# Order by hand held to the end of the second projection; copies of the last norm factors' rows and banks of the output product moved

## The chip, the cores and the metric

The kernel runs on one core of one Trainium2 chip. The metric is the device time of one execution in microseconds (us), the median of three runs. The engines in the profile: PE is TensorE (matmuls), PEld its weight loads, DVE is VectorE, ACT is ScalarE, POOL is GpSimd, SP is SyncE, which here issues DMAs.

## The reference

One layer that joins a gMLP mixer and a Mamba-2 mixer, in float32, with D = S = 1024 and one sequence. Its end, which the change touches, is:

```python
y_b = rms_norm(yz, ssm_norm_w.reshape(SSM_GROUPS, -1)).reshape(b, s, SSM_D_INNER)   # 2048 wide, 8 groups
merged = jax.nn.sigmoid(g_a) * (y_a @ w_proj_a) + jax.nn.sigmoid(g_b) * (y_b @ w_proj_b)
x = x + gate[:, None, :] * (merged @ w_out)
return rms_norm(x, final_norm_w)
```

## The kernel before

All of the product `y_b @ w_proj_b` is called the second projection here. It is done by seven products of half size (Strassen in Winograd's form) in the order p1, p2, p5, p3, p6, p7, p4. Each product runs over k = 0 to 7, and one pair (product, k) is a unit; `units` numbers them u = 0 to 55. A unit (`multiply`) is 12 matmuls of 128x128 by 128x512: four banks of PSUM, and on each bank the three parts of a product in split precision, where every operand is a high part (`bh`, a cast) and a low part (`bl`, what the cast left). p1, p6, p7 and p4 gather on the banks `x`, p2, p5 and p3 on the banks `y`; p3 goes on from p5's sums, and p6, p7 and p4 from what is in `x`.

After each unit `ahead(u)` issues the loads of unit u + 6 (on SP) and the operands of unit u + 4. `operands` makes the norm of a row block of y_b (`y_norm`, for p1, p2, p5 and p3), the differences that Winograd's form needs (`yn`), the cast to the high part on ScalarE and the low part on VectorE. `bh` and `bl` are rings of four, so the cast of unit u + 4 writes where unit u is read. When a product is done, its banks are copied or added to a sum (`c11`, `c`, p5's and p3's copies, and `p` in the trace for the sums that p6 and p7 are added to): p1's and p2's by `emptied_banks`, ahead of `ahead(u)`; the others at the loop's end, with high priority. From p3 on, every second unit has a `merged`: one piece of the merged rows from such a sum and two pieces loaded by `gate_load` (`tg`, `ma`), which ends as a high and a low part (`mh`, `ml`), operands of the output product. p4's banks are read by `merged` directly. During p7 and p4 pieces of w_out are loaded and split (`wo_load`, `wo_parts`).

VectorE, ScalarE and GpSimd run their instructions in the order in which the program has them after scheduling. While `hand[0]` is true, the wrapper class `Engine` pins each instruction to program order; when it is false, the scheduler orders by its own estimates. It is set true at the last pair of the input products and, before, false at u = 23, the end of p5. TensorE's matmuls of this projection are pinned in any case.

`post3` makes the norm factors' rows of one group pair: a transpose on TensorE into a bank of p2's set (`rows_bank`), a copy on VectorE (`cwt`, `tri`), and a store to `rs_d`, from which `y_load` reads rows (`rb`) for `y_norm`. In p1 it is called for groups 6 and 7.

`places_of` gives the banks of each set by `free`, the list of the banks in the order in which the work before gives them up; here it is [1, 7, 2, 3, 0, 4, 5, 6]. The pool `ps4` behind the loop has two tags: `pj` (two tiles of two banks, the output product's) and `one` (four tiles of one bank, its last row block). The output product starts with k = 4 to 7 and 0 to 3 (`KO`) on row blocks 4 and 5, whose operands are `merged`'s pieces (b, 1). `room` is the list of tags that `slot_tile` takes from the front.

Of the kernel before, what the change touches and what calls it, by code (L numbers as in the profile page):

```python
# [8 lines left out]
F32 = mybir.dt.float32  # L9
# [7 lines left out]
P = 128  # L17
D = 1024
S = 1024
KT = D // P  # L20
NCH = S // P
NG = 8
# [13 lines left out]
def hybrid_kernel(  # L36
# [7 lines left out]
    hand = [False]  # L44
# [13 lines left out]
    V, A, G, PE = Engine(nc.vector), Engine(nc.scalar), Engine(nc.gpsimd), nc.tensor  # L58
    ctx.enter_context(nc.allow_non_contiguous_dma(reason="small parameter vectors"))

    x, out = x[0], out[0]
# [33 lines left out]
    def f32(t):  # L95
        return t.bitcast(F32)
# [80 lines left out]
    with tc.tile_pool(name="p0", bufs=1, reuse_waits="tile") as p0:  # L177
# [257 lines left out]
        sums = {(6, 8): [(last_sums, 0)], (7, 2): [(last_sums, 1)], (7, 5): [(last_sums, 2)]}  # L435
# [47 lines left out]
    free, at_bank = [], {}  # L483
# [12 lines left out]
    def numbered(pool, c):  # L496
        for b in range(8):
            pool.tile([P, 512], F32, name=f"{c}{b}_0", tag=f"{c}{b}")
# [676 lines left out]
    groups = [Group(g) for g in range(NG)]  # L1175
# [36 lines left out]
    def ring(n):  # L1212

        return [room.pop(0) for _ in range(n)], [0]
# [20 lines left out]
    war_r, wah_r, wal_r = [], [], []  # L1235
# [144 lines left out]
    tha_r, ea_r, y1_r, ym_r = (ring(c) for c in (4, 3, 2, 2))  # L1380
# [59 lines left out]
    def banks(name, c):  # L1440
        return [psb.tile([P, 512], F32, name=f"{name}{j}", tag=f"q{places_of[c][j]}") for j in range(4)]
# [12 lines left out]
    def slot_tile(name, dt=F32):  # L1454
        tag = room.pop(0)
        t = hp.tile([P, 512], dt, name=name, tag=tag)
        tags_of[name] = tag
        return t

    def give(name):  # L1460
        room.append(tags_of.pop(name))
# [79 lines left out]
    def multiply(u, ps):  # L1541
        nm, k = units[u]
        first = nm in ("p1", "p2", "p5")
        a, (bh, bl) = aops.pop(u), bops.pop(u)
        for j in range(4):
            js = slice(j * P, (j + 1) * P)
            for n, (v, r) in enumerate(((0, bh), (0, bl), (1, bh))):
                pin(PE.matmul(ps[j], a[:, v, js], r, start=first and n + k == 0, stop=n == 2 and k == KT - 1,  # L1548
                              skip_group_check=not first))
# [3 lines left out]
    def gate_load(b, h):  # L1553
        hs = slice(h * 512, (h + 1) * 512)
        th, ma = gate_slot(f"tg{b}_{h}"), gate_slot(f"ma{b}_{h}")
        load(th, th_d[(KT + b) * P : (KT + b + 1) * P, hs])
        load(ma, mt_d[b][:, hs])
        gates[b, h] = th, ma
# [4 lines left out]
    def m_slot(name):  # L1563
        if m_sl:
            if not places:
                pool, b = m_sl.pop(0)
                t = pool.tile([P, 3, 512], F32R, name=f"m{name}", tag="sl", bufs=b)
                places.extend(t[:, i] for i in range(3))
            return places.pop(0)
        return places.pop(0) if places else slot_tile(name, F32R)  # L1570
# [6 lines left out]
    def merged(b, h, c, name):  # L1577

        th, ma = gates.pop((b, h))
        V.scalar_tensor_tensor(th, th, 1.0, c, op0=ALU.add, op1=ALU.mult)  # L1580
        V.tensor_add(th, th, ma)
        hi, lo = m_slot(f"mh{b}_{h}"), m_slot(f"ml{b}_{h}")
        if name:
            give(name)
        A.copy(hi, th)
        V.tensor_sub(lo, th, f32(hi))
        mhl[b, h] = hi, lo
# [3 lines left out]
    def ahead(u):  # L1591
        if u + LOAD < len(units):
            loads(u + LOAD)
        if u + LEAD < len(units):
            operands(u + LEAD)
# [3 lines left out]
    def ya_free():  # L1599

        while emptied[0] < KT and left[0] <= 3 * (KT - 1 - emptied[0]):
            room.extend(ya_tags[emptied[0]])
            emptied[0] += 1
# [3 lines left out]
    n = 0  # L1607
# [8 lines left out]
            loads(n - 1)  # L1616
    draw(left[0] + 1)
    ya_free()
    for tags in (war_r[0][0][:2], wah_r[0][0][2:], wal_r[0][0][2:], tha_r[0], y1_r[0], ym_r[0]):
        room.extend(tags)  # L1620
    ps2.__exit__(None, None, None)
    ps3 = tc.tile_pool(name="ps3", bufs=1, space=PSUM, reuse_waits="tile")
    psb = ps3.__enter__()
    numbered(psb, "q")
    places_of = {"x": free[:4], "y": free[4:]}
    wo, wor = {}, {}
    KO = (4, 5, 6, 7, 0, 1, 2, 3)

    def wo_load(k):
        wor[k] = [[slot_tile(f"wo{v}{k}_{c}", F32R) for v in "hl"] for c in range(2)]  # L1630
        for c in range(2):
            load(f32(wor[k][c][1]), wo_d[k][:, c * 512 : (c + 1) * 512])

    def wo_parts(k):
        for hi, lo in wor[k]:
            A.copy(hi, f32(lo))
            V.tensor_sub(lo, f32(lo), f32(hi))
        wo[k] = wor.pop(k)

    psx = psy = None  # L1640
    sums, more = [], []

    def emptied_banks(nm):
        for j in range(4):
            if nm == "p1":
                t = slot_tile(f"c11_{j}")
                A.copy(t, psx[j])
                more.append((j, 0, t, f"c11_{j}"))
            else:
                V.tensor_add(more[j][2], more[j][2], psy[j])  # L1650

    for u, (nm, k) in enumerate(units):
        if k == 0:
            if nm == "p1":
                psy = banks("yp2", "y")
                psx = banks("x", "x")
                rows_bank[0] = lambda name: psy[int(name[2:]) - 6]
            elif nm == "p5":
                psy = banks(f"y{nm}", "y")
            elif nm == "p6":  # L1660
                room.extend(rb_r[0])
            ps = psy if nm in ("p2", "p5", "p3") else psx
        multiply(u, ps)
        if u < 16 and k == KT - 1:
            emptied_banks(nm)
        ahead(u)
        if nm == "p1" and k in (4, 5):
            groups[NG - 6 + k].post3(True)
        if k % 2 and nm in GATES:
            gate_load(GATES[nm][0] + k // 2, GATES[nm][1])  # L1670
        if nm in ("p7", "p4") and k % 2 == 0:
            n = k // 2 + (4 if nm == "p4" else 0)
            kept = 2 * (16 - len(mhl)) - len(places) - 3 * len(m_sl)
            if len(room) >= 4 + kept and len(wor) + len(wo) < KT:
                wo_load(KO[len(wor) + len(wo)])
        if nm == "p4" and k % 2 and wor:
            wo_parts(next(iter(wor)))
        if k % 2 and more and u > 23:
            merged(*more.pop(0))
        if u == 23:  # L1680
            hand[0] = False
        if u > 15 and k == KT - 1:
            for j in range(4):
                with tc.high_priority():
                    if nm in ("p5", "p3"):
                        t = slot_tile(f"{nm}_{j}")
                        A.copy(t, psy[j])
                        sums.append(t)
                    elif nm == "p6":
                        V.tensor_add(sums[4 + j], sums[4 + j], psx[j])  # L1690
                        more.append((j, 1, sums[4 + j], f"p3_{j}"))
                    elif nm == "p7":
                        V.tensor_add(sums[j], sums[j], psx[j])
                        more.append((4 + j, 1, sums[j], f"p5_{j}"))
                    elif nm == "p4":
                        merged(4 + j, 0, psx[j], None)
    room.extend(bh_r[0] + bl_r[0])
    for n in KO:
        if n not in wo:
# [4 lines left out]


    ps4 = ctx.enter_context(tc.tile_pool(name="ps4", bufs=1, space=PSUM, reuse_waits="tile"))

    def pj_tile(name):
        return ps4.tile([P, 1024], F32, name=name, tag="pj", bufs=2)
# [4 lines left out]
    def inv_root(sq):  # L1714

        y, t, v = sq[:, 2:3], sq[:, 3:4], sq[:, 1:2]
        V.tensor_scalar(t, sq[:, 0:1], 1.0 / D, EPS, op0=ALU.mult, op1=ALU.add)
        V.tensor_scalar(y.bitcast(I32), t.bitcast(I32), -0.5, float(0x5F3759DF), op0=ALU.mult, op1=ALU.add)
        V.tensor_scalar_mul(v, t, -0.5)
        for _ in range(3):  # L1720
            V.scalar_tensor_tensor(t, y, y, v, op0=ALU.mult, op1=ALU.mult)
            V.scalar_tensor_tensor(y, t, 1.5, y, op0=ALU.add, op1=ALU.mult)
        return y
# [24 lines left out]
    for n, t in enumerate(tiles):  # L1748
# [22 lines left out]
        if last:  # L1771
            V.scalar_tensor_tensor(sq[:, 0:1], part[:, 0:1], part[:, 1:2], part[:, 2:3], op0=ALU.add, op1=ALU.add)
            y = inv_root(sq)
# [4 lines left out]
        else:  # L1778
            V.tensor_add(r, pw, xr)  # L1779
            A.activation(xr, r, AF.Square, accum_out=sq[:, 0:1])  # L1780
            y = inv_root(sq)
# [35 lines left out]
```

## Time and profile before

| | |
|---|---|
| time, median of 3 runs | 1432.4 us (1431.67 to 1433.11) |
| profiled execution | 1435.1 us |
| its span, first to last instruction | 1433.4 us |
| granted TensorE clock, mean | 0.995 |
| busy: PE, DVE, ACT, POOL | 97%, 72%, 54%, 14% |

The profiled execution has its own time, 2.7 us over the median; the rows of the profile belong to it. The second projection stands from about 1161 us to 1335 us of the span, the output product behind it. A matmul's row in the timeline gives start, length and in brackets the idle time before it with what ended that; a window's PEclk is the granted clock in that stretch, 1.00 for full speed.

### The profile page before, as it was taken

The numbers are of one execution on the slowest core, as the hardware profiler recorded it, in microseconds if no ns is written. First come the engines' busy times: TensorE is split into PE (matmuls) and PEld (weight loads), VectorE is DVE, ScalarE is ACT, GpSimd is POOL, SyncE is SP. The second block draws the span as 40 slices with busy tenths as digits, with TensorE's granted clock in tenths as the row PEclk, the third lists the DMA queues.
The fourth block names the chain that finished last, engine by engine and source line by source line (L and its number), as shares of the span: only waits on it lengthen the run. The fifth ranks groups of instructions, "written<-read, shape, count | busy, mean of one in ns | idle before, by whom it ended". The sixth has DMA issues, their size and how long they took to land.

```text
span 1433.4 us, 20485 instructions
## 1 busy us (share of the span) xinstructions
PE 1394.2 (97%) x7087; PEld 1152.3 (80%) x7087; DVE 1030.4 (72%) x1827; ACT 781.1 (54%) x1438; POOL 205.7 (14%) x190
## 2 busy tenths in 40 slices
PE   8999999999999999999999999999999998899997
PEld 6688888888888888888887888878888886687786
DVE  4686677777667888788877884768777757938443
ACT  6664576566656665555665555667767533325211
POOL 0000000000000000000010100048878820000000
PEclk9999999999999999999999999999999999999999
DMA  8552333333332677586676764789689488877331
GB/s 267 157 164 89 118 118 102 104 104 109 111 110 89 206 224 225 180 263 200 194 239 200 221 189 147 248 306 323 254 293 318 147 272 311 291 244 281 121 118 74
DMA packets 260524, 277.08 MB, mean 193 GB/s; under 512 B 13596, under 2 KB 210628, under 8 KB 260420
## 3 DMA queue, kind: packets, MB, share of 16 engines
q1 hardware_dynamic: 179396, 195.37, 43.3%
q10 hardware_dynamic: 81024, 80.40, 16.1%
q8 instruction: 56, 0.92, 0.2%
q14 instruction: 48, 0.39, 0.1%
HBM read 191.40 MB, written 84.31 MB: 192 GB/s over the span
## 4 chain that ended last, share of the span: by engine, by line
PE 77%; DMA 7%; DVE 7%; ACT 3%; issue 2%; POOL 2%; SPq 1%; ACTq 0%; POOLq 0%; DVEq 0%
PE xuz L585 6%; PE xcb L585 6%; PE po L90 6%; PE xx L585 6%; PE xz L585 5%; PE xg L585 5%; PE pma L90 3%; PE yuz L585 3%; PE xv L585 3%; PE ycb L585 3%; PE yx L585 3%; PE yp L1548 3%; PE yz L585 3%; PE yg L585 2%; PE yi L90 2%
## 5 line engine op out<-in xcount | busy, mean ns | idle before, releaser
L796 POOL TENSOR_TENSOR wog<-wog,gb 128x1024 f32<-128x1024 f32 x8 | 22.5, 2809 | 727.3 <-DMA wbr<-in_w_proj_b_dram 615.5
L56 ACT ACTIVATE dcy<-dcy,nacs 128x128 f32<-128x128 f32 x256 | 78.4, 389 | 34.4 <-POOL dcy L56 16.2
L56 POOL TENSOR_SCALAR_AFFINE_SELECT dcy<-dcy 128x1024 f32<-128x1024 f32 x32 | 37.4, 1169 | 106.0 <-ACT ea L56 105.9
L908 ACT ACTIVATE ac<-ac 128x1024 f32<-128x1024 f32 x32 | 34.0, 1062 | 20.2 <-DVE ac L906 20.1
L1780 ACT ACTIVATE xr<-r 128x1024 f32<-128x1024 f32 x7 | 7.4, 1061 | 66.8 <-issue 39.0
L90 PE MATMUL pma<-yh,wah 128*128 128x512 f32 x128 | 43.2, 419 | 0.1
L90 PE MATMUL pma<-yh,wal 128*128 128x512 f32 x128 | 42.8, 415 | 0.0
L56 DVE TENSOR_TENSOR ym<-yn,ea 128x512 f32<-128x512 f32 (+1 forms) x32 | 19.9, 623 | 30.2 <-PE yn L90 30.0
L56 POOL TENSOR_TENSOR yz<-y,sl 128x512 f32<-128x512 f32 x32 | 41.2, 1287 | 0.6
L56 ACT ACTIVATE ea<-dcy 64x512 f32<-64x512 f32 x64 | 40.2, 629 | 1.8 <-DMA dcy<-acs_d 1.3
L56 DVE TENSOR_TENSOR dcy<-dcy,pc 128x1024 f32<-128x1024 f32 x32 | 39.0, 1219 | 2.6 <-PE pc L93 1.4
L90 PE MATMUL pma<-yl,wah 128*128 128x512 f32 x128 | 40.0, 393 | 0.0
L1770 POOL TENSOR_TENSOR r<-r,fnw 128x256 f32<-128x256 f32 (+1 forms) x3 | 2.8, 917 | 254.2 <-ACT xr L1769 254.2
L56 POOL TENSOR_TENSOR y<-y,ym 128x512 f32<-128x512 f32 (+1 forms) x32 | 36.7, 1146 | 12.7 <-DVE ym L56 12.6
L906 DVE SCALAR_TENSOR_TENSOR ac<-c2x,cwt,ac 128x1023 f32<-128x1023 f32 (+2 forms) x24 | 31.8, 1325 | 9.0 <-ACT ac L904 7.1
L1779 DVE TENSOR_TENSOR r<-po,xr 128x1024 f32<-128x1024 f32 x7 | 8.6, 1225 | 41.2 <-PE po L90 41.1
L90 PE MATMUL yi<-dcy,xd 128*64 128x128 f32 x512 | 35.0, 279 | 0.9 <-DVE xe L56 0.6
L906 DVE SCALAR_TENSOR_TENSOR ac<-c2cb,cwt,ac 128x1023 f32<-128x1023 f32 (+2 forms) x24 | 30.6, 1275 | 7.1 <-ACT ac L904 7.0
L90 PE MATMUL sp<-xe,bn 128*128 128x256 f32 x112 | 32.7, 409 | 0.0
L90 PEld LDWEIGHTS yi<-dcy,xd 128*64 128x64 f32 x512 | 27.3, 136 | 5.3 <-issue 2.9
L906 DVE SCALAR_TENSOR_TENSOR ac<-c1cb,cwt,ac 128x1023 f32<-128x1023 f32 (+2 forms) x24 | 30.6, 1276 | 0.7 <-ACT ac L904 0.7
L906 DVE SCALAR_TENSOR_TENSOR ac<-c1x,cwt,ac 128x1023 f32<-128x1023 f32 (+2 forms) x24 | 30.6, 1277 | 0.0
(2847 smaller groups left out, 4400.2 us busy)
## 6 DMA issues: line engine op xcount, KB each, us to landing
sl<-s_d SPq DMA_DIRECT2D x32, 768.0 KB
s_d<-ac ACTq DMA_DIRECT2D x32, 512.0 KB
dcy<-acs_d SPq DMA_DIRECT2D x32, 512.0 KB
aw<-in_ada_w_dram SPq DMA_DIRECT2D x16, 512.0 KB
wbr<-in_w_proj_b_dram SPq DMA_DIRECT2D x64, 128.0 KB
wb_d<-wbb ACTq DMA_DIRECT2D x32, 256.0 KB
wb_d<-wbc ACTq DMA_DIRECT2D x32, 256.0 KB
yb_d<-yz ACTq DMA_DIRECT2D x32, 256.0 KB
```

The source lines that it names most:

```text
L56: return lambda *a, **k: tc.keep_in_program_order(f(*a, **k))
L90: pin(PE.matmul(acc, l, r, start=first, stop=last))
L585: pin(PE.matmul(ps, lw[:, k * P : (k + 1) * P], r[k], start=first and n + k == 0, stop=n == 2 and k == 3, skip_group_check=not first))
L796: G.tensor_mul(w, w, gb)
L906: V.scalar_tensor_tensor(ac[:, s:], cc[:, : S - s], conv_wt[:, 3 - s, i : i + 1], ac[:, s:], op0=ALU.mult, op1=ALU.add)
L908: A.activation(ac, ac, AF.Silu)
L1548: pin(PE.matmul(ps[j], a[:, v, js], r, start=first and n + k == 0, stop=n == 2 and k == KT - 1, skip_group_check=not first))
L1770: G.tensor_mul(r[:, cs], r[:, cs], fnw[:, cs])
L1779: V.tensor_add(r, pw, xr)
L1780: A.activation(xr, r, AF.Square, accum_out=sq[:, 0:1])
```

## The change

`hand[0]` stays true to the end of p4. All emptying of banks is now in `emptied_banks`, without high priority and ahead of `ahead(u)` for every product but p4, whose banks are emptied after the loop. `merged` is taken from the list ahead of the emptying and issued at the end of the unit. `post3` is called after p1's units k = 2 and 3, ahead of `ahead`. The banks are fixed: x is (1, 2, 3, 0) and y is 4 to 7. In `ps4` four tiles of the tag `one` are asked for first, which puts `pj` on banks 4 to 7. One group of tags goes to the end of `room`.

```diff
-    for tags in (war_r[0][0][:2], wah_r[0][0][2:], wal_r[0][0][2:], tha_r[0], y1_r[0], ym_r[0]):
+    for tags in (war_r[0][0][:2], wah_r[0][0][2:], wal_r[0][0][2:], y1_r[0], ym_r[0], tha_r[0]):
...
-    places_of = {"x": free[:4], "y": free[4:]}
+    places_of = {"x": (1, 2, 3, 0), "y": range(4, 8)}
...
             else:
-                V.tensor_add(more[j][2], more[j][2], psy[j])
+                merged(4 + j, 0, psx[j], None)
...
         multiply(u, ps)
-        if u < 16 and k == KT - 1:
+        if nm == "p1" and k in (2, 3):
+            groups[NG - 4 + k].post3(True)
+        due = more.pop(0) if k % 2 and more and u > 23 else None
+        if k == KT - 1 and nm != "p4":
             emptied_banks(nm)
         ahead(u)
-        if nm == "p1" and k in (4, 5):
-            groups[NG - 6 + k].post3(True)
...
-        if k % 2 and more and u > 23:
-            merged(*more.pop(0))
-        if u == 23:
-            hand[0] = False
-        if u > 15 and k == KT - 1:
-            for j in range(4):
-                with tc.high_priority():
...
+        if due:
+            merged(*due)
+    emptied_banks("p4")
+    hand[0] = False
...
+    for n in range(4):
+        ps4.tile([P, 512], F32, name=f"one{n}_0", tag="one", bufs=4)
```

The branches of the removed block for p5, p3, p6 and p7 stand unchanged in `emptied_banks`, together with p2's.

On VectorE around the operands of p3's k = 2 and 3 (`p3bl_12000` is the low part of k = 2; `yn` rows are norms and differences, those of line 1520, 1534 and 1523 belong to p6 and p7), before:

```order
L1580 SCALAR_TENSOR_TENSOR tg_0_12024<-tg_0_12024,c_3_11620 128x512
L1534 TENSOR_TENSOR yn_0_11508<-yn_0_11508,yn_1_11721 128x512
L1523 TENSOR_TENSOR yn_0_11249<-yn_1_11721,yn_0_11249 128x512
L1520 TENSOR_TENSOR yn_1_11818<-yn_1_12015,yn_1_11818 128x512
L1487 SCALAR_TENSOR_TENSOR yn_1_12050<-yn_1_12050,par_140,rb_1_12048 128x512
L1520 TENSOR_TENSOR yn_1_11746<-yn_1_11946,yn_1_11746 128x512
L1534 TENSOR_TENSOR yn_0_11590<-yn_0_11590,yn_1_11792 128x512
L1523 TENSOR_TENSOR yn_0_11327<-yn_1_11792,yn_0_11327 128x512
L56 TENSOR_TENSOR p3bl_12000<-yn_1_11946,p3bh_11999 128x512
```

And after, at the same place:

```order
L56 TENSOR_TENSOR p3bl_11973<-yn_1_11918,p3bh_11972 128x512
L56 SCALAR_TENSOR_TENSOR yn_1_11946<-yn_1_11946,par_140,rb_1_11944 128x512
L56 TENSOR_TENSOR p3bl_12000<-yn_1_11946,p3bh_11999 128x512
L56 SCALAR_TENSOR_TENSOR yn_1_11967<-yn_1_11967,par_140,rb_1_11944 128x512
L56 TENSOR_TENSOR p3bl_12029<-yn_1_11967,p3bh_12028 128x512
```

Before, differences of p6 and p7 and a step of `merged` stand between the norm and the low part of a p3 unit; after, norm and low part stand side by side, and the others come later.

On VectorE at the end of p6 (`p` with `x` are the adds that empty p6's banks, `p7bl` the low parts of p7's operands, the first three for k = 0 to 2), before:

```order
L1527 TENSOR_TENSOR p7bl_12329<-yn_0_11244,p7bh_12328 128x512
L1527 TENSOR_TENSOR p7bl_12348<-yn_0_11249,p7bh_12347 128x512
L1690 TENSOR_TENSOR p_0_12217<-p_0_12217,x_11416 128x512
L1527 TENSOR_TENSOR p7bl_12371<-yn_0_11256,p7bh_12370 128x512
L1690 TENSOR_TENSOR p_1_12219<-p_1_12219,x_11417 128x512
```

And after:

```order
L56 TENSOR_TENSOR yn_0_11672<-yn_0_11672,yn_1_11868 128x512
L56 TENSOR_TENSOR yn_0_11244<-yn_1_11698,yn_0_11244 128x512
L56 TENSOR_TENSOR p7bl_12329<-yn_0_11244,p7bh_12328 128x512
L56 TENSOR_TENSOR yn_0_11249<-yn_1_11721,yn_0_11249 128x512
L56 TENSOR_TENSOR p7bl_12348<-yn_0_11249,p7bh_12347 128x512
L56 TENSOR_TENSOR yn_0_11256<-yn_1_11746,yn_0_11256 128x512
L56 TENSOR_TENSOR p7bl_12371<-yn_0_11256,p7bh_12370 128x512
L56 TENSOR_TENSOR p_0_12204<-p_0_12204,x_11416 128x512
L56 TENSOR_TENSOR p_1_12206<-p_1_12206,x_11417 128x512
L56 TENSOR_TENSOR p_2_12208<-p_2_12208,x_11418 128x512
L56 TENSOR_TENSOR p_3_12210<-p_3_12210,x_11419 128x512
```

The differences that p7 needs stand now right ahead of its low parts, six instructions of p7's k = 0 to 2 are ahead of the first add, and the four adds stand together.

On VectorE in p1, the difference of the two orders where the rows of groups 6 and 7 are copied (`cwt`, `tri`):

```order
+L56 COPY cwt<-yp_11412 8x128
 L56 SCALAR_TENSOR_TENSOR yn_0_11434<-yn_0_11434,par_140,rb_0_11432 128x512
-L56 TENSOR_TENSOR p1bl_11491<-yn_0_11434,p1bh_11490 128x512
+L56 TENSOR_TENSOR p1bl_11494<-yn_0_11434,p1bh_11493 128x512
 L56 TENSOR_TENSOR p1a_11436<-p1r_11437,p1a_11436 128x512
+L56 COPY tri<-yp_11413 8x128
 L56 SCALAR_TENSOR_TENSOR yn_0_11458<-yn_0_11458,par_140,rb_0_11432 128x512
```

The two copies stand now ahead of the operands of p1's k = 6 and 7; before, they stood behind those of p2's k = 0 and 1.

More of the change, by code (lines that the diff above doesn't have):

```diff
@@ L1624, in hybrid_kernel @@
     numbered(psb, "q")
-    places_of = {"x": free[:4], "y": free[4:]}
+    places_of = {"x": (1, 2, 3, 0), "y": range(4, 8)}
+    assert all(b > 3 for b in free[6:])
     wo, wor = {}, {}
@@ L1648, in emptied_banks @@
                 more.append((j, 0, t, f"c11_{j}"))
+            elif nm == "p2":
+                V.tensor_add(more[j][2], more[j][2], psy[j])
+            elif nm in ("p5", "p3"):
+                t = slot_tile(f"{nm}_{j}")
+                A.copy(t, psy[j])
+                sums.append(t)
+            elif nm == "p6":
+                V.tensor_add(sums[4 + j], sums[4 + j], psx[j])
+                more.append((j, 1, sums[4 + j], f"p3_{j}"))
+            elif nm == "p7":
+                V.tensor_add(sums[j], sums[j], psx[j])
+                more.append((4 + j, 1, sums[j], f"p5_{j}"))
             else:
-                V.tensor_add(more[j][2], more[j][2], psy[j])
+                merged(4 + j, 0, psx[j], None)
     for u, (nm, k) in enumerate(units):
@@ L1677, in hybrid_kernel @@
             wo_parts(next(iter(wor)))
-        if k % 2 and more and u > 23:
-            merged(*more.pop(0))
-        if u == 23:
-            hand[0] = False
-        if u > 15 and k == KT - 1:
-            for j in range(4):
-                with tc.high_priority():
[L1685 to L1696, printed above, removed]
+        if due:
+            merged(*due)
+    emptied_banks("p4")
+    hand[0] = False
     room.extend(bh_r[0] + bl_r[0])
```

## The prediction

> **What bounds the kernel now.** I read first the head of the page, then the waits of TensorE in the last third of the span, then TensorE's timeline at each of these waits, and last VectorE's timeline just before them.
>
> ```profile
> span 1433.4 us, 20485 instructions
> PE 1394.2 (97%) x7087; PEld 1152.3 (80%) x7087; DVE 1030.4 (72%) x1827; ACT 781.1 (54%) x1438; POOL 205.7 (14%) x190
> ```
>
> TensorE is busy for 97% of the span: it sets the time, and what can be won is its idle time and the stretches at half clock. The waits of TensorE from 1100 us on (total, times, longest):
>
> ```profile
> PE yp L1548 <- DVE p3bl L56: 6.7, 3, 4.3
> PE yp L1548 <- issue: 4.4, 1, 4.4
> PE po L90 <- DVE tg L1580: 2.2, 1, 2.2
> PE yp L1548 <- DVE tri L56: 1.9, 1, 1.9
> PE x L1548 <- DVE p L1690: 0.6, 2, 0.4
> ```
>
> They sum to 15.8 us, nearly all of them VectorE's doing. TensorE's timeline has them at these places (start, duration, engine, line, operation; in brackets the idle time before it):
>
> ```profile
> 1161.63 0.39 PE L1548 MATMUL x<-p1bh,p1a 128*128 128x512 f32 x1
> 1163.44 0.61 PE L1548 MATMUL x<-p1bh,p1a 128*128 128x512 f32 x2
> 1166.16 0.61 PE L1548 MATMUL x<-p1bh,p1a 128*128 128x512 f32 x2
> 1186.61 0.50 PE L1548 MATMUL yp<-p2bh,p2a 128*128 128x512 f32 x1 [1.88 <-DVE tri L56]
> 1212.37 0.76 PE L1548 MATMUL yp<-p5bh,p5a 128*128 128x512 f32 x1 [4.37 <-issue]
> 1246.35 0.80 PE L1548 MATMUL yp<-p3bl,p3a 128*128 128x512 f32 x1 [4.33 <-DVE p3bl L56]
> 1253.10 0.79 PE L1548 MATMUL yp<-p3bl,p3a 128*128 128x512 f32 x1 [2.17 <-DVE p3bl L56]
> 1268.20 0.39 PE L1548 MATMUL x<-p6bh,p6a 128*128 128x512 f32 x1
> 1289.96 0.39 PE L1548 MATMUL x<-p7bh,p7a 128*128 128x512 f32 x1
> 1312.93 0.39 PE L1548 MATMUL x<-p4bh,p4a 128*128 128x512 f32 x1
> 1335.28 0.39 PE L90 MATMUL po<-woh,mh 128*128 128x512 f32 x1
> 1339.00 0.50 PE L90 MATMUL po<-woh,mh 128*128 128x512 f32 x1 [2.20 <-DVE tg L1580]
> ```
>
> From 1163.44 to 1166.16 run 12 matmuls, one unit: 2.72 us, and a product of eight units 21.76 us undisturbed. p6 shows just that (1268.20 to 1289.96). p7 takes 22.97 and p4 22.35. The windows behind three of the gaps, and behind the one of 1.88 (length; busy time and count of PE, PEld, DVE, ACT, POOL; granted clock; DMA share; GB/s):
>
> ```profile
> 1212.20:1215.60 3.40, 3.23 (x8) 2.58 (x9) 3.22 (x6) 0.04 (x1) 0.00 (x0) 0.50 1.03 410
> 1246.30:1249.70 3.40, 3.35 (x8) 2.67 (x9) 3.40 (x6) 1.22 (x2) 0.00 (x0) 0.50 0.01 4
> 1253.10:1256.50 3.40, 3.40 (x8) 2.72 (x9) 3.40 (x6) 0.00 (x0) 0.00 (x0) 0.50 0.10 42
> 1184.80:1188.20 3.40, 1.59 (x7) 1.33 (x8) 2.36 (x5) 1.63 (x4) 0.00 (x0) 1.00 0.47 144
> ```
>
> So a long gap costs itself and 1.7 us more, half of 3.4 us at half clock; the gap of 1.88 us drew no such stretch, that of 2.17 us did.
>
> **The prices on VectorE.**
>
> ```profile
> 1165.74 0.15 DVE L56 TENSOR_SCALAR ssq<-pq 128x4 f32<-128x4 f32 x1
> 1186.28 0.27 DVE L56 COPY tri<-yp 8x128 f32<-8x128 f32 x1
> 1208.75 0.75 DVE L56 SCALAR_TENSOR_TENSOR yn<-yn,par,rb 128x512 f32<-128x512 f32 x1
> 1209.53 0.69 DVE L56 TENSOR_TENSOR yn<-yn,yn 128x512 f32<-128x512 f32 x1
> 1210.98 0.69 DVE L56 TENSOR_TENSOR p5bl<-yn,p5bh 128x512 fp32r<-128x512 f32 x1 [0.76 <-ACT p5bh L56]
> 1211.59 2.48 DVE L56 TENSOR_TENSOR c<-c,yp 128x512 f32<-128x512 f32 x4
> 1213.98 0.75 DVE L56 SCALAR_TENSOR_TENSOR yn<-yn,par,rb 128x512 f32<-128x512 f32 x1
> 1243.81 0.68 DVE L1520 TENSOR_TENSOR yn<-yn,yn 128x512 f32<-128x512 f32 x1
> 1244.41 0.69 DVE L1534 TENSOR_TENSOR yn<-yn,yn 128x512 f32<-128x512 f32 x1
> 1245.61 0.69 DVE L56 TENSOR_TENSOR p3bl<-yn,p3bh 128x512 fp32r<-128x512 f32 x1
> ```
>
> From start to start: a p5 unit (norm, difference, wait for ScalarE's cast, low part) 2.84 us (1208.75 to 1211.59); a p3 unit without one step of 0.78 then 2.06; the four adds that empty a set of banks 2.39 (1211.59 to 1213.98), the first after some 0.7; one more plain difference 0.60 (1243.81 to 1244.41). A p6 unit (difference, cast, low part, difference) is 2.66 and a p7 unit 2.06, a p4 unit (the low part alone) 0.6. A `merged` (two steps, cast, low part) has a p5 unit's shape: 2.84. These are estimates from the rows above.
>
> **The change part by part.** The rows of groups 6 and 7 move from p1's k = 4, 5 to k = 2, 3, two units sooner and ahead of the operands of p1's k 6 and 7 instead of behind those of p2's k 0 and 1. The copy of `tri` at 1186.28, for which p2 finds one of its banks still unread, then comes about 5 us sooner, and the wait of 1.88 us goes. In its place p1's fourth bank is now bank 0, last read by VectorE at 1165.74 to 1165.89, while p1 comes to it 9 matmuls, 2.04 us, after its start at 1161.63: a new wait of some 2.2 us (1165.9 less 1163.67). Neither counts: p5 starts when VectorE's adds at 1211.59 have emptied the first bank, and these stand behind the operands of p5's k 0 to 2 as before; p2's end, 4.37 us ahead, has room for either. Were that cover gone, 0.3 us would be the net. Worth 0, and the 4.37 us gap with its half clock stays. The stores of these rows go out sooner too, and SP, which now stands 7.9 us for one of them ahead of the row loads, stands shorter; TensorE waits for none of those loads, so this is worth 0 as well.
>
> ```profile
> SPq L99 <- DMA rs_d<-cwt: 7.9, 1, 7.9
> 1298.97 6.92 DMA p4a<-wb_d
> SPq L99 <- DVE tg L1581: 12.9, 2, 8.8
> ```
>
> The copies that empty p5's banks, on ScalarE, also lose their priority and stand behind the casts of p3's k 0 to 2. The last of these waits for p5's k 6 to end, 2.72 us before the copies can begin, so ScalarE is free by then; 0, at most the 0.6 of one cast.
>
> p3 is the gain. Its low parts now wait behind p6's and p7's differences, the rows before 1245.61; in the new order each p3 unit has its norm and its low part side by side. The cast of unit u + 4 waits for TensorE's end of unit u (a ring of four), so VectorE is done some 1.5 us after that, about 6 us ahead of need. p3 shrinks from 32.5 us (1235.7 to 1268.20, the start being p5's 1212.37 + 1.7 + 21.76) to 21.8: −10.7 us. It starts p6 at about 1257.6.
>
> VectorE is then late. p3's k 1 ends at 1212.37 + 1.7 + 10 × 2.72 = 1241.3, so k 5's operands end at 1242.8. What stands behind them in order: merged to 1245.6, p3's k 6 and 7 to 1249.8, merged to 1252.6, p6's k 0 and 1 to 1257.9, merged to 1260.8, k 2 and 3 to 1266.1, merged to 1268.9. TensorE ends p6's k 3 at 1257.6 + 4 × 2.72 = 1268.4, and k 4's low part is ready 2.06 later than 1268.9, at 1271.0: a wait of 2.4 in two pieces. From there VectorE's 2.66 a unit keeps TensorE's 2.72, and p6 ends at 1281.7 or 1281.9: +2.5 us.
>
> The second new wait is larger. The four adds that empty p6's banks stood among p7's operands as soon as p6 had ended (waits of 0.6 us in all); they now stand behind p7's k 0 to 2. VectorE ends p6's k 7 at 1268.9 + 4 × 2.66 = 1279.6, these three at 1285.7, the first add at 1286.45. TensorE idles 4.5 us from 1281.9, which by the rows of 4.37 and 4.33 us brings half clock for 3.4 us: +1.7. p7 then takes 21.76 + 1.7 instead of 22.97, and ends at 1309.9. Together p6's end to p4's start becomes 28.3 us against 22.97: +5.4 us.
>
> [...]
>
> p7 to p4: the ring lets p7's k 5 go at p7's k 1 end, 1293.6; then merged, k 6 and 7, merged, two p4 units, merged and a third p4 unit, from 1295.0 by the prices above to 1297.8, 1301.9, 1304.7, 1306.0, 1308.8 and 1309.4. The adds follow at once, first done at 1310.1: a wait of 0.3 us where p4 now has small ones. p4 starts at 1310.2 and ends at 1332.0, 21.85 us against 22.35: −0.5.
>
> The output product waits 2.20 us at 1339.00 for the product of line 1580 that reads one of p4's banks. On banks y, last read after p3, nothing is to wait for: −2.4 us with the matmuls behind it counted in step (1339.00 − 6 × 0.227 = 1337.64 as undisturbed start, less 1335.28). The next thing late would be the last merged operand of the half that it starts with; its tg and ma come in p7, its sums at 1312, and TensorE asks for it three units after 1332.0, at 1340: some us to spare. From there to the end nothing changes.
>
> Sum: −10.7 + 2.5 + 5.4 − 0.5 − 2.4 = −5.7, and by the chain of times 1332.0 against 1337.64, **−5.6 us**. The profiled execution took 1435.1 us, 2.7 over the median of 1432.4; it becomes 1429.5, and the median **1426.8**. The adds, copies and DMAs themselves are the same in number, only their places differ.
>
> Not shown in the trace: what VectorE takes for this very order. Bounds from the nearest rows: p5bl waited 0.76 us for its cast, a row in p2 1.03, which over the four units and merges that matter in p6 makes VectorE about 1 us later; below, the plain low parts in p3 started 0.60 after the step before them, with the cast hidden, which makes it 2 to 3 us sooner. I take 0.76, the same engines in the same queue order.
>
> ```profile
> 1190.96 0.69 DVE L56 TENSOR_TENSOR p2bl<-yn,p2bh 128x512 fp32r<-128x512 f32 x1 [1.03 <-ACT p2bh L56]
> ```
>
> **The rivals.** *VectorE keeps up.* With casts hidden, the adds come 2.5 us sooner, the gap of 4.5 is 2.0 and draws no half clock: −5.6 − 2.5 − 1.7 = −9.8, 1422.6. For it: rows 1244.41 to 1245.61 at 0.60 each. Against: there the scheduler had put other work between cast and low part, here each low part stands right behind its own cast.
>
> *Half clock twice.* p6's gap of 2.4 us acts as the one of 2.17 did, +1.7, and VectorE is 1.0 later: −2.9, 1429.5. For it the window at 1253.10; against it those at 1.88 and, in the output product, 2.20 us, whose matmul of 0.50 is not at half speed.
>
> *Slower: SP's queue.* SP issues p4's operands in one line with the loads of the gates, and the gates' slots are given back by `merged`, which now keeps its place in VectorE's order.
>
> The rows of SP above show that it has stood 8.8 us for such a slot, and that a row of p4 took 6.92 us to land. By the times above the slots come at about 1304.7, 1308.8 and, behind the adds, 1315.2; p4's k 2, 4 and 6, queued behind them, land at 1311.6, 1315.7 and 1322.1, needed at 1315.6, 1321.1 and 1326.6. From a landing of 10.5 us on (or merges 3.5 us later) each pair of units waits: three gaps of about 3.5 with two half clocks, +14 against the forecast's −5.6 is +8.4, 1440.8. Against it: 4 us of room at each.
>
> *The change does less than it says.* The rows sooner bring nothing at p5's start; that is in the forecast at 0.
>
> **How the numbers follow.** About 0.2%, 2.9 us, is what a measurement of this kernel tells from no change; the line is at 1429.5. Forecast 0.73; VectorE keeps up 0.11; half clock twice 0.10, of which 0.02 on the faster side; slower 0.06. Faster: 0.73 + 0.11 + 0.02 = 0.86; same 0.08; slower 0.06. The range goes from short of the first rival, 1423.3 (most of the cast's wait hidden), to just behind the second, 1430.3; outside lie SP's queue and about all of the first rival, 0.17.
>
> **What would show it.** In the changed profile: no wait of p3 for p3bl, p6 at about 1257.6, a gap of about 2 us in p6's middle for p6bl, one of 4 to 5 us ahead of p7 (by the adds at line 1656) with a window at 0.50, p7 to p4 nearly without a gap, no wait for tg in the output product, and p5 still at about 1212.4 behind a gap of over 4. Waits for p4a, or a p3 that still waits, would prove it wrong.

## The result, and the profile after

The kernel after takes 1429.4 us (median; 1427.4 to 1432.5) where the kernel before, on the same chip, took 1432.9: a ratio of 0.9977 with an interval of 0.9968 to 0.9987, that is 1.9 to 4.6 us faster. Timed once more on another occasion it was 0.9971 (0.9961 to 0.9981). The forecast was 5.6 us, with the sign and the range right; the measured gain is three fifths of it. The head of the page of the profiled execution:

```profile
span 1428.1 us, 20481 instructions
PE 1392.1 (97%) x7087; PEld 1152.1 (81%) x7087; DVE 1035.0 (72%) x1827; ACT 780.3 (55%) x1438; POOL 206.0 (14%) x190
```

TensorE's waits from 1100 us on (total, times, longest):

```profile
PE yp L1548 <- issue: 6.4, 1, 6.4
PE x L1548 <- issue: 3.4, 2, 2.8
PE x L1548 <- ACT p6bh L56: 1.3, 1, 1.3
PE x L1548 <- DVE ssq L56: 1.1, 1, 1.1
PE po L90 <- DVE r L1780: 0.6, 1, 0.6
...
PE x L1548 <- DVE p6bl L56: 0.2, 1, 0.2
```

The waits for `p3bl`, `tg` and `tri` are gone; new are one for `ssq` in p1, one in the middle of p6 and two ahead of p7 and p4 ("issue"). TensorE's timeline has them here:

```profile
1164.30 0.50 PE L1548 MATMUL x<-p1bh,p1a 128*128 128x512 f32 x1 [1.10 <-DVE ssq L56]
1212.74 0.77 PE L1548 MATMUL yp<-p5bh,p5a 128*128 128x512 f32 x1 [6.41 <-issue]
1258.98 0.39 PE L1548 MATMUL x<-p6bh,p6a 128*128 128x512 f32 x1
1271.31 0.50 PE L1548 MATMUL x<-p6bh,p6a 128*128 128x512 f32 x1 [1.29 <-ACT p6bh L56]
1272.04 0.50 PE L1548 MATMUL x<-p6bl,p6a 128*128 128x512 f32 x1 [0.22 <-DVE p6bl L56]
1287.43 0.47 PE L1548 MATMUL x<-p7bh,p7a 128*128 128x512 f32 x1 [2.81 <-issue]
1310.03 0.47 PE L1548 MATMUL x<-p4bh,p4a 128*128 128x512 f32 x1 [0.56 <-issue]
1331.92 0.39 PE L90 MATMUL po<-woh,mh 128*128 128x512 f32 x1
```

What "issue" stands for is read from VectorE's timeline at those places: the four adds that empty p2's and p6's banks, and the row ahead of each.

```profile
1211.35 0.69 DVE L56 TENSOR_TENSOR p5bl<-yn,p5bh 128x512 fp32r<-128x512 f32 x1 [0.76 <-ACT p5bh L56]
1211.96 2.48 DVE L56 TENSOR_TENSOR c<-c,yp 128x512 f32<-128x512 f32 x4
1286.04 0.69 DVE L56 TENSOR_TENSOR p7bl<-yn,p7bh 128x512 fp32r<-128x512 f32 x1 [0.76 <-ACT p7bh L56]
1286.65 2.47 DVE L56 TENSOR_TENSOR p<-p,x 128x512 f32<-128x512 f32 x4
```

The first add of p6's begins at 1286.65, straight behind p7's third low part, and TensorE at 1287.43, when that add has ended.

### The profile page after: what moved, and what is told of

It reads as the page before. It is cut to its first block, busy times and chain, and to the rows that moved or that the text cites. A ratio compares the mean times of both kernels' runs of the same rounds, so it can differ in the third digit from the quotient of the medians.

```text
span 1428.1 us, 20481 instructions
## 1 busy us (share of the span) xinstructions
PE 1392.1 (97%) x7087; PEld 1152.1 (81%) x7087; DVE 1035.0 (72%) x1827; ACT 780.3 (55%) x1438; POOL 206.0 (14%) x190
## 4 chain that ended last, share of the span: by engine, by line
PE 68%; DMA 11%; DVE 9%; ACT 5%; issue 3%; POOL 3%; SPq 1%; ACTq 0%; POOLq 0%; DVEq 0%
PE xuz L585 6%; PE xcb L585 6%; PE xx L585 5%; PE xz L585 5%; PE po L90 4%; PE xg L585 4%; PE yuz L585 3%; PE xv L585 3%; PE ycb L585 3%; PE yz L585 2%; PE yg L585 2%; PE yx L585 2%; PE pma L90 2%; PE yp L1548 2%; PE yv L585 2%
## 5 line engine op out<-in xcount | busy, mean ns | idle before, releaser
L56 DVE SCALAR_TENSOR_TENSOR y<-sl,dskt,yi 128x256 f32<-128x256 f32 x64 | 27.7, 473 | 4.0 <-POOL yz L56 2.8
```

The source lines that it names most:

```text
L56: return lambda *a, **k: tc.keep_in_program_order(f(*a, **k))
```

## The experiments

In each table or sentence the ratio is that of the kernel's time to the kernel before, with its interval. Line numbers in rows of changed kernels are their own.

**The other parts without the order.** The kernel before with `post3` sooner, the fixed banks, the output product's banks and the order of `room`.

```diff
...
-    places_of = {"x": free[:4], "y": free[4:]}
+    places_of = {"x": (1, 2, 3, 0), "y": range(4, 8)}
...
+        if nm == "p1" and k in (2, 3):
+            groups[NG - 4 + k].post3(True)
...
+    for n in range(4):
+        ps4.tile([P, 512], F32, name=f"one{n}_0", tag="one", bufs=4)
```

> The kernel before with the other parts of the change alone: rows of groups 6 and 7 copied earlier, banks x = (1,2,3,0) and y = 4 to 7, output product on banks y, tags of room; the order by hand ends at p5 as before. If the gain is VectorE's order in p3, p3's waits of 4.3 and 2.2 us with their half clock stay, no new wait comes in p6 or ahead of p7, and only the output product's wait goes: 1 to 2.4 us faster than before, ratio 0.998 to 0.999. If the gain comes from rows and banks: as the whole change, ratio 0.9977 or lower, with p3 unchanged.

Measured: 0.9997 (0.9986 to 1.0008). TensorE's timeline:

```profile
1166.34 0.50 PE L1548 MATMUL x<-p1bh,p1a 128*128 128x512 f32 x1 [1.34 <-DVE ssq L56]
1214.09 0.77 PE L1548 MATMUL yp<-p5bh,p5a 128*128 128x512 f32 x1 [5.70 <-issue]
1249.51 0.79 PE L1548 MATMUL yp<-p3bl,p3a 128*128 128x512 f32 x1 [4.33 <-DVE p3bl L56]
1256.25 0.50 PE L1548 MATMUL yp<-p3bl,p3a 128*128 128x512 f32 x1 [1.46 <-DVE p3bl L56]
```

p3's waits stay, with no wait in p6 or in the output product. The parts by themselves bring nothing that can be measured, less than either expectation. In the profile the output product has its gain (95.6 us from its first matmul to the span's end, 98.1 before), but the median does not show it.

**The order without the other parts.** The kernel after with rows, banks, output product's banks and tags of before.

```diff
...
-    places_of = {"x": (1, 2, 3, 0), "y": range(4, 8)}
...
+    places_of = {"x": free[:4], "y": free[4:]}
...
-    for n in range(4):
-        ps4.tile([P, 512], F32, name=f"one{n}_0", tag="one", bufs=4)
```

> The order by hand to the end of p4 and the new places of the emptying alone; rows, banks, output product's banks and tags as before. By the sum of the prediction: all but the 2.4 us of the output product, 3 us faster than before. Rival: once the order is held, the output product, which then starts on p4's banks, must wait until the merges that read them have come up in program order behind all other VectorE work, some 6 us for the first tile and 7 for the second: 7 to 11 us slower than before, ratio 1.005 to 1.008, and the change of banks is what makes the held order usable.

Measured: 1.0102 (1.0079 to 1.0126), 14.6 us slower: the rival, and more than its 7 to 11 us. p3 has no wait, p6 has the 1.3 and 0.2 us, 4.4 stand ahead of p7, and two long waits are in the output product (TensorE's timeline, then the VectorE row that ends the first of the two):

```profile
1284.92 0.76 PE L1548 MATMUL x<-p7bh,p7a 128*128 128x512 f32 x1 [4.38 <-issue]
1337.84 0.80 PE L90 MATMUL po<-woh,mh 128*128 128x512 f32 x1 [6.54 <-DVE tg L56]
1348.30 0.79 PE L90 MATMUL po<-woh,mh 128*128 128x512 f32 x1 [7.53 <-DVE tg L56]
```

```profile
1337.11 0.68 DVE L56 SCALAR_TENSOR_TENSOR tg<-tg,x 128x512 f32<-128x512 f32 x1
```

`merged` reads the first of p4's banks only at 1337.11, behind the merges of the other half and w_out's low parts, and the output product's first matmul follows at 1337.84; on the banks y no run shows a wait for `tg`. About half of the 14.6 us is half clock: the mean granted clock of its runs makes a loss of 15.6 us over the span, that of the runs of before 8.5. So the held order is worth its gain only together with the other parts, and the waits point to the output product's banks: alone the two are +14.6 and about 0, together −3.4.

**p6's last difference into the wait for the cast.** The kernel after with one VectorE instruction per p6 unit moved ahead of the low part.

```diff
         keep(A.copy(hi, t))
+        if nm == "p6":
+            V.tensor_sub(b21, b21, b12)
         keep(V.tensor_sub(lo, t, f32(hi)))
...
-        if nm == "p6":
-            V.tensor_sub(b21, b21, b12)
-        elif nm == "p7":
+        if nm == "p7":
```

> The kernel after with one instruction per p6 unit moved: the difference that p4 needs is issued between cast and low part instead of behind the low part. If VectorE's 2.66 us a unit in p6 set the waits in the middle of p6 and ahead of p7, a unit becomes 2.06, the middle wait with its half clock goes (1.5 + 1.7 us) and the gap ahead of p7 shrinks to 1 to 2.5 us: 3.5 to 4.8 us faster than after, ratio to before 0.9943 to 0.9953. If loads or ScalarE set them: as after, 0.9977.

Measured: 0.9937 (0.9919 to 0.9955), some 5.7 us faster than after, a little more than expected. p6 runs from 1260.7 us to p7's start without a wait but the one ahead of p7:

```profile
1284.76 0.47 PE L1548 MATMUL x<-p7bh,p7a 128*128 128x512 f32 x1 [2.04 <-issue]
```

VectorE's pace in p6 was what set the wait in its middle; 0.6 us in each of eight units is enough. Ahead of p7 2.0 us stay, where three units of p7 still stand ahead of the adds.

**The adds ahead of p7's k = 2.**

```diff
+    held = []
...
-        ahead(u)
+        if u + LOAD < len(units):
+            loads(u + LOAD)
+        if nm in ('p6',) and k >= KT - 1 - 1 and k < KT - 1:
+            held.append(u + LEAD)
+        else:
+            held.append(u + LEAD)
+            while held:
+                v = held.pop(0)
+                if v < len(units):
+                    operands(v)
```

> The kernel after with the operands of p7's k = 2 issued behind the four adds that empty p6's banks, instead of ahead of them. If the gap of 2.8 us ahead of p7 is these adds' place in VectorE's order, it shrinks by one p7 unit, 2.06 us, to about 0.7, of which up to 1.3 us comes back as a longer wait ahead of p4, where the operands are late by as much: 0.8 to 2 us faster than after, ratio to before 0.9963 to 0.9972. If p7's loads set it: unchanged.

Measured: 0.9981 (0.9967 to 0.9994), no faster than after.

```profile
1284.73 0.47 PE L1548 MATMUL x<-p7bh,p7a 128*128 128x512 f32 x1 [0.79 <-issue]
1309.39 0.76 PE L1548 MATMUL x<-p4bh,p4a 128*128 128x512 f32 x1 [2.59 <-ACT p4bh L56]
```

The gap ahead of p7 shrank by the 2.0 us expected and came back ahead of p4, 2.6 us with half clock behind it (its first matmul takes 0.76 us). Where VectorE was the one that was late here, a new order of its work moved the wait (2.0 us less ahead of p7, 2.6 us ahead of p4); work put into its own waits removed one (p6's 1.5 us in the experiment before).

**The next unit's norm into the wait for the cast.** The kernel after, from u = 4 on:

```diff
         keep(A.copy(hi, t))
+        if u >= 4:
+            norm_of(u + 1)
         keep(V.tensor_sub(lo, t, f32(hi)))
```

`norm_of` makes a unit's `y_norm` if it is not made yet.

> The kernel after with the norm of the next unit issued between a unit's cast and its low part, from p1's k = 5 on, so that VectorE works where it waited 0.76 us for each cast. If VectorE's pace (2.72 us a unit in p2, 2.84 in p5) set the start of p5, as the prediction says, the gap of 4.4 to 6.4 us ahead of p5 shrinks to under 1 us and its half clock goes, p6's middle and the gap ahead of p7 stay as in after: 6 to 9 us faster than after, ratio to before 0.991 to 0.9935. If loads or the store of the rows of groups 6 and 7 set it: as after, 0.9977.

Measured: 0.9912 (0.9897 to 0.9927), 9 us faster than after. p5's rows, whose longest matmul was 767 ns in after (granted clock 0.50 from 1212.00 to 1215.40 us), and the gap ahead of p7:

```profile
L1556 PE MATMUL yp<-p5bh,p5a x64: 389/389/389, 1210.0 to 1231.5; 128*128 128x512 f32 x64
1280.45 0.77 PE L1556 MATMUL x<-p7bh,p7a 128*128 128x512 f32 x1 [4.40 <-issue]
```

There is no wait ahead of p5 any more: the 4.4 us that the kernel before had there, and the 3.0 to 6.4 of the kernel after, were VectorE's pace in p2 and p5, and neither loads nor the rows of groups 6 and 7.

**Both moves.**

> Both moves into the wait for the cast: the next unit's norm, and in p6 the difference that p4 needs. If each gap is VectorE's pace, the gains add: the gap ahead of p5 goes, p6's middle too, and ahead of p7 and p4 about 1 us each stays: 10 to 14 us faster than after, ratio to before 0.988 to 0.991. If something else is late next (rows of y_b or p3's weights from SP, which were never asked for so early): 6 us faster than after at most, ratio 0.9935.

Measured: 1416.3 us, 0.9866 (0.985 to 0.9883), somewhat better than expected, and faster than before by about 19 us and than after by 16. About 7.6 of the 19 us are half clock: the mean granted clock is 0.999 in each of these runs and 0.992 to 0.995 in those of before on that occasion, a loss of 1.4 us over the span against 9.0. Two rows of VectorE in p2, whose unit there is now 1.87 us from start to start, and what is left of waits in the projection:

```profile
1185.62 0.68 DVE L56 TENSOR_TENSOR p2bl<-yn,p2bh 128x512 fp32r<-128x512 f32 x1
1187.49 0.68 DVE L56 TENSOR_TENSOR p2bl<-yn,p2bh 128x512 fp32r<-128x512 f32 x1
```

```profile
1167.32 0.50 PE L1556 MATMUL x<-p1bh,p1a 128*128 128x512 f32 x1 [1.46 <-DVE ssq L56]
1275.40 0.47 PE L1556 MATMUL x<-p7bh,p7a 128*128 128x512 f32 x1 [0.68 <-issue]
1298.02 0.47 PE L1556 MATMUL x<-p4bh,p4a 128*128 128x512 f32 x1 [0.58 <-issue]
```

**And p7's next difference too.**

```diff
             norm_of(u + 1)
+            p7_diff(u + 1)
```

`p7_diff` makes the difference of a p7 unit if it is not made yet.

> As the kernel with both moves into the wait for the cast, and p7's next difference moved there too. p7's unit on VectorE goes from 2.06 to about 1.4 us, and the gaps of 0.68 us ahead of p7 and 0.58 ahead of p4 go: 1 to 1.5 us faster than that kernel, ratio to before 0.9855 to 0.9862. If ScalarE's casts or p4's rows are late next: no change, 0.9866.

Measured: 0.9868 (0.9852 to 0.9883), no change, though p7 and p4 now start without a wait. 1.3 us is near what one comparison tells, and p1 of this profile had a stretch at half clock (1.7 us lost) behind a wait of 1.80 us for `ssq`, so whether the move brings its 1 us stays open.

**The rows late again.** The kernel after with `post3` at its old place.

> The kernel after with the copies of the rows of groups 6 and 7 back at their old place, behind the operands of p2's k = 0 and 1. By the prediction the earlier rows are worth 0, since p5's start is set by VectorE: a wait for tri of 0.5 to 2 us at p2 comes on top of the new one for ssq in p1, the gap ahead of p5 is that much shorter, and the time is as after, ratio to before 0.9965 to 0.9988. If the rows' move is a gain of its own: 1.9 us slower than after, ratio 0.999.

Measured: 0.9954 (0.9942 to 0.9967), lower than expected, so it was run once more beside the kernel after:

> The kernel after with the rows of groups 6 and 7 copied late, beside the kernel after on the same chip. If the rows' move is worth 0, the two ratios agree within 0.0015. If it costs, by the wait for ssq that p1 then shows earlier and a stretch at half clock behind it, this one is lower by 0.002 as it was in the run apart.

> The kernel after, timed on the same chip as the one with late rows: ratio to before 0.9968 to 0.9987 as first measured, if neither chip nor session matters; 0.996 if the first comparison was high by chance.

Measured: 0.9966 (0.9953 to 0.9979) with late rows and 0.9971 (0.9961 to 0.9981) for the kernel after. Side by side they agree: the earlier rows are worth nothing that can be measured, and the first 0.9954 was probably low by chance.

**Both kernels profiled again.**

> The kernel before, profiled again: do the places and sizes of the waits (1.9 at p2, 4.4 ahead of p5, 4.3 and 2.2 in p3, 2.2 in the output product) repeat, and the stretches at half clock behind them? If the stretches hang on where a gap falls, their number differs; p1's start, ahead of which both kernels are the same, shows how far a single profile scatters.

> The kernel after, profiled again: p5 50 to 52 us behind p1's start, p3 without a gap, 1.5 us in p6, 3 to 4.5 us ahead of p7. Half clock behind p6's small gap and none ahead of p7, as in the first profile, or the other way round, as the prediction has it.

The spans: before 1433.4 and 1434.8 us; after 1428.1, 1427.2 and (from the last comparison) 1431.6. The gaps repeat within some tenths, but for those ahead of p5 and p7; the stretches at half clock do not repeat. They are told below.

## Why the prediction was right, and where its sizes were off

**p3, −10.7 us: right.** p3 runs without a wait in every kernel that has the held order, and keeps its waits where only the other parts are done.

**The two new waits, +2.5 and +5.4 us: the mechanism right, the half clock in the other place.** VectorE reached p6's k = 4 and the adds about as worked out: the adds were forecast to start at 1285.7 and started at 1286.65. The middle of p6 waited 1.5 us and drew the half clock (granted clock 0.51 from 1272.85 to 1276.26 us), and ahead of p7 the gap of 2.8 us drew none (1.00 from 1286.50 to 1289.91). From p6's start to p4's the forecast had 52.6 us (1257.6 to 1310.2), 7.9 more than before (1268.20 to 1312.93); it took 51.05 (1258.98 to 1310.03), 6.3 more. In the profile of the last comparison it is the other way round, as forecast: the gap ahead of p7 is 4.40 us with half clock, and p6's, of 1.29 and 0.23 us, has none (granted clock 1.00 from 1270.70 to 1277.50 us).

```profile
1289.84 0.77 PE L1548 MATMUL x<-p7bh,p7a 128*128 128x512 f32 x1 [4.40 <-issue]
```

In the second profile both drew half clock (1.7 us lost in p6 and 3.4 in p7; longest matmul of p6 628 ns, of p7 764 ns), which is the rival of half clock twice. The sum counts no half clock behind p6's gap. No run shows that as a rule: before, the gaps of 1.88 and 2.20 us drew none and that of 2.17 us did, and p6's gap drew one in two of the three profiles of after.

The rival in which VectorE keeps up did not come, since waits of 0.7 to 0.8 us for the cast stand ahead of the low parts of p5, p6 and p7; the experiments that fill them are that rival made true. The rival of SP's queue did not come either: no wait for p4's rows appears.

**p4 and the output product, −0.5 and −2.4 us: right.** The product starts at 1331.92, forecast 1332.0, and has no wait for `tg`; from there to the span's end it takes 96.2 us, and 95.7 and 95.6 in the other profiles of after, against 98.1 and 99.4 before. That the start is met within 0.1 us is luck: p6 began 1.4 us late, and p6 to p4 took 1.55 us less than forecast.

**p1 to p5, worth 0: mis-sized.** p5's start came 51.7 us behind p1's in the first profile of after and 50.9 and 52.9 in the others, 50.7 and 50.3 in those of before (the distances of the first matmuls of p1 and p5). The new wait for `ssq` is 1.1 to 1.8 us early in p1, and in two of three profiles a stretch at half clock follows it (1.7 us lost in each). The ring of four ties the casts to TensorE's units, so a delay there can reach p5's start in part. By the means of these five profiles it is 1.3 us, but they scatter by 2; the experiments on the same banks that leave the norms in place lie at 48.7 to 51.5, and the held order on the old banks at 49.7. That the cause is bank 0 in x was not tried alone and stays open.

**The half clock, counted at −1.7 us: wrong.** The forecast had three stretches before and two after. The profiles lose to it between 1155 and 1345 us, as the sum of one less the granted clock over windows of 1 us: 5.1 and 8.5 us before, 5.1, 10.2 and 6.8 after. Both kernels have several gaps of 1.1 to 3 us, of which some drew one (2.17 us before, p6's 1.5 after) and some did not (1.88 and 2.20 us before, 2.81 after). The two profiled executions differ by 5.3 us, all but the forecast, since both happened to lose 5.1; the medians, taken over executions in which the stretches fall differently, differ by 3.4 and 3.8, and the ratios give 3.3 and 4.2. The runs themselves say more than the profiles, since each has its span and mean granted clock on record (the clock to 0.001, which is 1.4 us in one run and averages out over many). In the last comparison the ten runs of after lose 8.9 us to half clock over the span and the fourteen of before 8.7: nothing saved, where 1.7 us was forecast (standard error 0.7). Without that loss the spans differ by 4.0 us (standard error 0.6), and the forecast without its half clock is 3.9. So there the half clock is the term that made the sum too large; p5's later start is in part the same loss, since the stretches behind `ssq` lie in it. For the first comparison the clocks of before's runs are not on record.

## What to carry to other kernels

When one engine prepares what another consumes through a short ring, price the producer's unit from start to start, waits for a third engine included, and compare it with the consumer's: here 2.84 us in p5, and 2.66 with a `merged` behind every second unit in p6's first four, against 2.72, made a gap where other work was queued. A better order largely moved such a gap here (p3's 10.7 us came back as 6.3 in p6 and p7); work put into the producer's own waits (0.76 us for each cast) removed it, and was worth over four times the change itself. An order held by hand can depend on a second decision, here, by the waits, the banks on which the next product starts: the order alone was +14.6 us, and the other parts alone nothing.

## What the runs showed of the hardware

In the profiles the stretches at half clock between 1155 and 1345 us begin whole steps of 3.41 us apart: before at 1212.16, 1246.29 and 1253.12 (10 and 2 steps), after at 1211.41 and 1272.85 (18 steps); the steps of the two lie 0.75 us apart. In ten of the profiles, the two of before and the three of after among them, 27 such stretches were read: 22 lost 1.7 us each and 5 lost 3.4, one or two steps at 0.50. The kernel after, cut in its steps (length; busy time and count of PE, PEld, DVE, ACT, POOL; granted clock; DMA share; GB/s):

```profile
1208.00:1211.41 3.41, 0.00 (x0) 0.00 (x0) 2.11 (x4) 1.09 (x2) 0.00 (x0) 1.00 0.96 321
1211.41:1214.82 3.41, 2.08 (x5) 1.73 (x6) 3.41 (x6) 0.00 (x0) 0.00 (x0) 0.51 1.00 396
1214.82:1218.23 3.41, 3.41 (x9) 2.65 (x9) 2.58 (x5) 0.62 (x1) 0.00 (x0) 0.50 0.73 235
1269.44:1272.85 3.41, 1.89 (x8) 1.02 (x7) 2.65 (x5) 0.62 (x1) 0.00 (x0) 1.00 0.93 337
1272.85:1276.26 3.41, 3.41 (x10) 2.65 (x9) 2.23 (x4) 0.93 (x2) 0.00 (x0) 0.51 0.19 76
1283.09:1286.50 3.41, 1.53 (x7) 0.94 (x5) 1.89 (x4) 1.24 (x2) 0.00 (x0) 1.00 0.70 264
1286.50:1289.91 3.41, 2.48 (x11) 2.07 (x12) 3.23 (x6) 0.07 (x1) 0.00 (x0) 1.00 0.00 0
```

A step in which TensorE idled for 1.52 us was followed by half clock (1269.44), one with 1.88 us was not (1283.09): the gap of 2.81 us lay across two steps, with 1.88 and 0.93 us. And a step at half clock with 1.33 us of idle time (1211.41) was followed by another. From 1155 to 1345 us of the first profiles of before and after, cut so, the full-speed steps with 3.41, 3.41 and 2.17 us of idle time before and 3.41 us after were followed by half clock; of those with 1.75 and 1.65 us before and 1.67, 1.52 and 1.88 us after only that of 1.52 us was; and of the others, all with under 1.2 us, none. The first run with late rows has a stretch (1.7 us lost, from 1159.2 us on) behind a step with 0.97 us, in which eight matmuls of one column (`pq`) follow the idle time:

```profile
1157.67 1.05 PE L90 MATMUL pq<-ones,sq 128*128 128x1 f32 x8 [0.97 <-POOL sq L56]
```

So these profiles show no single amount of idle time behind which half clock comes.

What a gap cost beyond itself was 0, 1.7 or 3.4 us here. The kernel before shows such a difference on two occasions: in the output product its gap of 2.20 us drew nothing (granted clock 1.00 from 1334.97 to 1341.79), and that of 1.90 us in the second profile did:

```profile
1335.92:1339.33 3.41, 1.51 (x7) 0.97 (x6) 3.41 (x7) 0.62 (x1) 0.00 (x0) 1.00 0.76 276
1339.33:1342.74 3.41, 3.41 (x10) 2.63 (x9) 3.41 (x7) 1.84 (x3) 0.00 (x0) 0.50 0.01 4
```

Nor did a gap of some 4.5 us cost 1.7 us beyond itself each time, as the prediction has it. The gap of 4.40 us in the profile of the last comparison lay with 2.38 and 2.02 us in two steps, and each step was followed by half clock, 3.4 us in all:

```profile
1284.41:1287.82 3.41, 1.03 (x5) 0.53 (x3) 2.52 (x4) 0.64 (x2) 0.00 (x0) 1.00 0.45 178
1287.82:1291.24 3.42, 1.40 (x3) 1.16 (x4) 2.79 (x5) 0.60 (x1) 0.00 (x0) 0.50 0.00 0
1291.24:1294.65 3.41, 3.41 (x9) 2.64 (x8) 2.19 (x4) 0.62 (x1) 0.00 (x0) 0.50 0.00 0
```
